# Re-cutting the loads of an in-place channel shuffle: 4, 8, 16, 32 KB in one shared buffer first, 4 KB last

## Chip, cores and metric

One Trainium2 (trn2) chip, one core. The time is the device time of the kernel in microseconds, median over several executions; the times of one kernel mostly differ by some tenths of a per cent, those of the kernel before by up to 1%. The profiler's span, from the first to the last instruction, is about 1.8 us shorter than the timed value of the same execution.

## The reference

The input is 67 MB of float32. Each group of 256 channels is seen as 8 groups of 32 and transposed to 32 times 8. Nothing is computed; every byte is read once and written once.

```python
x = x.reshape(batch, h, w, groups, channels_per_group)   # 16, 64, 64, 8, 32
x = x.transpose(0, 1, 2, 4, 3)
x = x.reshape(batch, h, w, c)
```

## The kernel before

Sizes are rows of 256 floats per partition, so 1 KB each: `16` is 16 KB per partition, 2 MB over 128 partitions. A load fills one of three buffers of 64 KB per partition. DVE (VectorE) copies 8 KB at a time into PSUM, another on-chip memory, in the shuffled order, and ACT (ScalarE) copies it back into the same place. After each 32 KB (or at the end of a smaller load) a store goes out from the same buffer. Loads are issued by SP (SyncE), stores by ACT.

```python
_SIZES = [16, 32] + [64] * 7 + [16]
_BUFS = 3
_STORE = 32
_PIECE = 8
...
    for q in _SIZES:
        buf = pool.tile([P, biggest * c], F32, name="buf")
        nc.sync.dma_start(out=buf[:, : q * c], in_=rows(x_flat, first, q))
        for a in range(0, q, _STORE):
            b = min(a + _STORE, q)
            for k in range(a, b, _PIECE):
                piece = buf[:, k * c : (k + _PIECE) * c]
                bounce = psum.tile([P, _PIECE * c], F32, name="bounce")
                nc.vector.tensor_copy(...)          # shuffle into PSUM
                nc.scalar.copy(out=piece, in_=bounce)
            cols = slice(a * c, b * c)
            nc.scalar.dma_start(
                out=rows(out_flat, first, q)[:, cols], in_=buf[:, cols]
            )
        first += P * q
```

Of the kernel before, what the change touches and what calls it, by code (L numbers as in the profile page):

```python
# [1 line left out]

# [4 lines left out]


F32 = mybir.dt.float32
P = 128  # L10

_SIZES = [16, 32] + [64] * 7 + [16]
_BUFS = 3

_STORE = 32

_PIECE = 8


@with_exitstack  # L20
def kernel(
    ctx: ExitStack,
    tc: tile.TileContext,
    x: bass.AP,
    groups: bass.AP,
    out: bass.AP,
):
    nc = tc.nc
    n, h, w, c = x.shape
    G = int(groups)  # L30
    CPG = c // G
    assert G * CPG == c
    assert sum(_SIZES) * P == n * h * w
    biggest = max(_SIZES)

    x_flat = x.rearrange("b h w c -> (b h w c)")
    out_flat = out.rearrange("b h w c -> (b h w c)")

    pool = ctx.enter_context(tc.tile_pool(name="pool", bufs=_BUFS))
    psum = ctx.enter_context(  # L40
        tc.tile_pool(name="psum", bufs=2, space=bass.MemoryType.PSUM)
    )

    def rows(flat, first, q):

        return flat[first * c : (first + P * q) * c].rearrange("(p f) -> p f", p=P)

    ctx.enter_context(tc.manual_schedule(engines=None))
    first = 0
    for q in _SIZES:  # L50
        buf = pool.tile([P, biggest * c], F32, name="buf")
        nc.sync.dma_start(out=buf[:, : q * c], in_=rows(x_flat, first, q))  # L52
        for a in range(0, q, _STORE):
            b = min(a + _STORE, q)
            for k in range(a, b, _PIECE):
                piece = buf[:, k * c : (k + _PIECE) * c]
                bounce = psum.tile([P, _PIECE * c], F32, name="bounce")
                nc.vector.tensor_copy(  # L58
                    out=bounce.rearrange("p (i j g) -> p i j g", j=CPG, g=G),
                    in_=piece.rearrange("p (i g j) -> p i j g", g=G, j=CPG),  # L60
                )
                nc.scalar.copy(out=piece, in_=bounce)  # L62
            cols = slice(a * c, b * c)
            nc.scalar.dma_start(
                out=rows(out_flat, first, q)[:, cols], in_=buf[:, cols]
            )
        first += P * q


# [1 line left out]
_INS = ['x', 'groups']  # L71
_OUTS = [((16, 64, 64, 256), 'float32')]

_NUMBERS = {'groups': 8}


# [26 lines left out]
```

## Time and profile before

| | before |
|---|---|
| time, median of 3 | 317.65 us (317.52 to 317.97) |
| span of the profiled execution | 317.3 us (that execution was timed at 319.09) |
| DVE / ACT busy | 227.8 / 120.6 us |
| DMA queues, share of 16 engines | 49.6% loads + 49.0% stores |
| bytes moved | 134.24 MB |

### The profile page before, as it was taken

The numbers are of one execution on the slowest core, as the hardware profiler recorded it, in microseconds if no ns is written. First come the engines' busy times: TensorE is split into PE (matmuls) and PEld (weight loads), VectorE is DVE, ScalarE is ACT, GpSimd is POOL, SyncE is SP. The second block draws the span as 40 slices with busy tenths as digits, with TensorE's granted clock in tenths as the row PEclk, the third lists the DMA queues.
The fourth block names the chain that finished last, engine by engine and source line by source line (L and its number), as shares of the span: only waits on it lengthen the run. The fifth ranks groups of instructions, "written<-read, shape, count | busy, mean of one in ns | idle before, by whom it ended". The sixth has DMA issues, their size and how long they took to land.

```text
span 317.3 us, 235 instructions
## 1 busy us (share of the span) xinstructions
DVE 227.8 (72%) x64; ACT 120.6 (38%) x65; POOL 0.2 (0%) x4
## 2 busy tenths in 40 slices
DVE  0979039993999999915999069990799807999600
ACT  0444205552444455421544215442245502455500
POOL 0000000000000000000000000000000000000000
DMA  8998999999999999999999999999999999999995
GB/s 318 413 492 361 456 397 413 446 401 463 401 500 413 401 442 417 508 397 409 430 483 417 397 443 409 475 392 442 439 479 397 425 438 413 446 430 434 438 417 231
DMA packets 3890, 134.24 MB, mean 423 GB/s; under 512 B 432, under 2 KB 432, under 8 KB 432
## 3 DMA queue, kind: packets, MB, share of 16 engines
q1 hardware_dynamic: 1440, 67.11, 49.6%
q10 hardware_dynamic: 2448, 67.11, 49.0%
q14 instruction: 2, 0.02, 0.0%
HBM read 67.11 MB, written 67.11 MB: 423 GB/s over the span
## 4 chain that ended last, share of the span: by engine, by line
DMA 56%; DVE 22%; another core or an unknown queue 12%; ACT 2%; DVEq 1%; issue 1%; SPq 0%
DMA buf<-in_x_dram 34%; DMA out_dram<-buf 22%; DVE bounce L58 22%; ACT buf L62 2%; DVEq L98 1%; SPq L52 0%; DVEq L58 0%
## 5 line engine op out<-in xcount | busy, mean ns | idle before, releaser
L58 DVE COPY bounce<-buf 128x2048 f32<-128x2048 f32 x64 | 227.8, 3637 | 71.2 <-DMA buf<-in_x_dram 71.2
L62 ACT COPY buf<-bounce 128x2048 f32<-128x2048 f32 x64 | 119.4, 1865 | 171.8 <-DVE bounce L58 171.8
L62 ACT ACT_TABLE_LOAD x1 | 1.3, 1283 | 8.4 <-DMA buf<-in_x_dram 8.4
L84 POOL MEMSET const-uint8-127<- 128x1 uint8 x1 | 0.1, 102 | 0.0
L84 POOL MEMSET const-bfloat16-1.0<- 128x1 bf16 x1 | 0.1, 101 | 0.0
L84 POOL MEMSET const-float32-0.0<- 128x1 f32 x1 | 0.1, 98 | 0.2 <-issue 0.2
L84 POOL MEMSET const-float32-1.0<- 128x1 f32 x1 | 0.1, 98 | 0.0
## 6 DMA issues: line engine op xcount, KB each, us to landing
out_dram<-buf ACTq DMA_DIRECT2D x15, 4096.0 KB, 40.4
buf<-in_x_dram SPq DMA_DIRECT2D x2, 2048.0 KB, 13.1
buf<-in_x_dram SPq DMA_DIRECT2D x1, 4096.0 KB, 16.9
out_dram<-buf ACTq DMA_DIRECT2D x2, 2048.0 KB, 21.5
buf<-in_x_dram SPq DMA_DIRECT2D x7, 33.4
```

The source lines that it names most:

```text
L58: nc.vector.tensor_copy(out=bounce.rearrange("p (i j g) -> p i j g", j=CPG, g=G), in_=piece.rearrange("p (i g j) -> p i j g", g=G, j=CPG),)
L62: nc.scalar.copy(out=piece, in_=bounce)
L84: nc = _bacc.Bacc("TRN2", target_bir_lowering=False, num_devices=1)
L98: with _tile.TileContext(nc) as tc:
```

## The change

The intent: begin computing sooner (a 4 KB load lands sooner than one of 16 KB), spend no buffer of its own on each small load, and end with a small piece, so that little is left to compute and store after the last load.

```diff
-_SIZES = [16, 32] + [64] * 7 + [16]
+_SLOTS = [[4, 8, 16, 32]] + [[64]] * 7 + [[4]]
...
-    for q in _SIZES:
+    for parts in _SLOTS:
         buf = pool.tile([P, biggest * c], F32, name="buf")
-        nc.sync.dma_start(out=buf[:, : q * c], in_=rows(x_flat, first, q))
...
+        at = 0
+        pieces = []
+        for q in parts:
+            pieces.append((q, first, at))
+            nc.sync.dma_start(
+                out=buf[:, at * c : (at + q) * c], in_=rows(x_flat, first, q)
+            )
+            first += P * q
+            at += q
+        for q, start, at in pieces:
+            for a in range(0, q, _STORE):
+                b = min(a + _STORE, q)
+                for k in range(a, b, _PIECE):
+                    m = min(_PIECE, b - k)
...                     # the same two copies, of m rows
```

Loads go from 10 to 12 and stores from 17 to 19. The fourth buffer use must now wait for all four stores of the first buffer.

More of the change, by code (lines that the diff above doesn't have):

```diff
@@ L32 @@
     assert G * CPG == c
-    assert sum(_SIZES) * P == n * h * w
-    biggest = max(_SIZES)
+    assert sum(map(sum, _SLOTS)) * P == n * h * w
+    biggest = max(map(sum, _SLOTS))
     x_flat = x.rearrange("b h w c -> (b h w c)")
@@ L49 @@
     first = 0
-    for q in _SIZES:
+    for parts in _SLOTS:
         buf = pool.tile([P, biggest * c], F32, name="buf")
-        nc.sync.dma_start(out=buf[:, : q * c], in_=rows(x_flat, first, q))
-        for a in range(0, q, _STORE):
-            b = min(a + _STORE, q)
-            for k in range(a, b, _PIECE):
-                piece = buf[:, k * c : (k + _PIECE) * c]
-                bounce = psum.tile([P, _PIECE * c], F32, name="bounce")
-                nc.vector.tensor_copy(
-                    out=bounce.rearrange("p (i j g) -> p i j g", j=CPG, g=G),
-                    in_=piece.rearrange("p (i g j) -> p i j g", g=G, j=CPG),
-                )
-                nc.scalar.copy(out=piece, in_=bounce)
-            cols = slice(a * c, b * c)
-            nc.scalar.dma_start(
-                out=rows(out_flat, first, q)[:, cols], in_=buf[:, cols]
-            )
-        first += P * q
+        at = 0
[12 more added lines that the diff above has]
+                    m = min(_PIECE, b - k)
+                    piece = buf[:, (at + k) * c : (at + k + m) * c]
+                    bounce = psum.tile([P, _PIECE * c], F32, name="bounce")
+                    bounce = bounce[:, : m * c]
+                    nc.vector.tensor_copy(
+                        out=bounce.rearrange("p (i j g) -> p i j g", j=CPG, g=G),
+                        in_=piece.rearrange("p (i g j) -> p i j g", g=G, j=CPG),
+                    )
+                    nc.scalar.copy(out=piece, in_=bounce)
+                nc.scalar.dma_start(
+                    out=rows(out_flat, start, q)[:, a * c : b * c],
+                    in_=buf[:, (at + a) * c : (at + b) * c],
+                )
 _INS = ['x', 'groups']
```

## The prediction

> **What bounds the kernel now.** I read the page's share of each engine first, then its strip of 40 slices with the DMA queues, then the chain that ended last, then the waits of the queue that issues loads, and last the busy share of the DMA engines in short windows at both ends.
>
> The page, busy shares, strip and queues:
>
> ```profile
> span 317.3 us, 235 instructions
> DVE 227.8 (72%) x64; ACT 120.6 (38%) x65; POOL 0.2 (0%) x4
> ...
> DMA  8998999999999999999999999999999999999995
> ...
> DMA packets 3890, 134.24 MB, mean 423 GB/s; under 512 B 432, under 2 KB 432, under 8 KB 432
> ...
> q1 hardware_dynamic: 1440, 67.11, 49.6%
> q10 hardware_dynamic: 2448, 67.11, 49.0%
> ```
>
> No compute engine is the bound: DVE is idle for 28% of the span. The DMA strip is full from the first slice to the last but one. The two queues' packets (q1 the loads, q10 the stores) take 49.6 + 49.0 = 98.6% of 16 engines' time, 312.9 us of 317.3. What is not filled is 317.3 - 312.9 = 4.4 us. While busy the engines move 134.24 MB / 312.9 us = 429 GB/s. The kernel has to read 67.11 MB and write 67.11 MB whatever the order, so this number is what the change must be held against.
>
> The chain that ended last names other things too: waits for DVE appear in it with 22%. Its first lines, columns start in us, length in us, what:
>
> ```profile
> 0.73 7.63 DMA buf<-in_x_dram
> 8.36 0.02 issue
> 8.38 7.16 DVE bounce L58 x2
> ...
> 17.46 27.51 DMA out_dram<-buf
> 44.97 0.02 issue
> 44.99 0.03 SPq L52
> ```
>
> This is latency of one small item, and not work that the chip lacked. The 2 MB store issued at 17.46 took 27.51 us to land because it shared the engines with loads already queued. Only then did its buffer come free for the fourth load. The waits of the load queue say the same, 263.3 us in seven waits for stores to land:
>
> ```profile
> SPq L52 <- DMA out_dram<-buf: 263.3, 7, 45.5
> ```
>
> A wait of a queue is a cost only if the DMA engines run dry during it. So the ends decide. Windows, with columns start:end and length, busy DVE, ACT, POOL, clock, DMA share, GB/s:
>
> ```profile
> 0.00:2.00 2.00, 0.00 (x0) 0.00 (x0) 0.20 (x4) 1.00 0.61 115
> 2.00:3.00 1.00, 0.00 (x0) 0.00 (x0) 0.00 (x0) 1.00 0.35 82
> ...
> 4.00:5.00 1.00, 0.00 (x0) 0.00 (x0) 0.00 (x0) 1.00 1.11 475
> ...
> 300.00:305.00 5.00, 0.00 (x0) 0.88 (x1) 0.00 (x0) 1.00 1.05 452
> 305.00:307.00 2.00, 0.00 (x0) 0.00 (x0) 0.00 (x0) 1.00 0.95 410
> ...
> 312.00:313.00 1.00, 0.00 (x0) 0.00 (x0) 0.00 (x0) 1.00 1.03 442
> 313.00:314.00 1.00, 0.00 (x0) 0.00 (x0) 0.00 (x0) 1.00 0.50 213
> 314.00:315.00 1.00, 0.00 (x0) 0.00 (x0) 0.00 (x0) 1.00 0.15 66
> ```
>
> A packet is booked whole where it begins, which is why a share can pass 1.00; I read neighbours together. Compute ends at 300.9 us, when the last 2 MB store is issued. Yet the DMA stays full to 313, twelve microseconds more: about 12.1 x 0.429 = 5.2 MB were still to be moved, of which only 2.1 MB belong to that last store. The tail is a backlog of stores, not an exposed last computation. After 313 only stragglers of the 16 engines remain: the last store's sixteen completions in the trace are spread from 313.8 to 316.4, median 314.1. At the head the first packet starts at 1.72 us.
>
> **What the Trainium skill says.** "DMA: Bandwidth & Descriptors", section "Where 436 GB/s comes from", gives 435.2 GB/s as the ceiling of the 16 ports. The 429 GB/s above is 98.5% of it. "HBM Reference", section "Specifications (TRN2)", says that a core streaming alone measures about 425 GB/s, bounded by its 16 DMA engines; the trace's 423 over the span agrees. "DMA: Bandwidth & Descriptors", section "Queues, rings and completion order", says that each engine takes the queues that have work in turn, one packet at a time. The trace agrees: a packet here is one partition's row, with 8 rows per engine and transfer. The packet records show 0.611 us for 16 KB, 1.213 for 32 KB and 2.418 for 64 KB. Eight 16 KB store packets taken in turn with 64 KB load packets need 8 x (0.611 + 2.418) = 24.2 us, and the store above took 27.51. So in this kernel loads get two thirds of the engines when both queues are full (64 KB against 32 KB), and stores lag.
>
> **The change, part by part.**
>
> *Bytes.* Unchanged: 67.11 MB each way.
>
> *Packets.* Sixteen KB more cost 1.213 - 0.611 = 0.602 us, so 0.611 - 0.602 = 0.009 us of a packet lies beside its bytes. Loads go from 10 to 12 transfers and stores from 17 to 19. That is 4 more transfers of 128 rows and 16 completions each: 512 data packets and 64 completions (recorded at 0.009 us each). On 16 engines: 576 x 0.009 / 16 = 0.32 us more.
>
> *Compute.* DVE now has 63 copies of 128x2048 and two of 128x1024, the same elements and one instruction more. DVE stays near 228 us and ACT near 121, both far below 313. One instruction's fixed cost is hidden.
>
> *Head.* Six loads are issued in a row at some 0.33 us each, 188 KB per partition, 24.6 MB, which is 57 us of DMA work. The first load of 0.5 MB lands near 3.5 us instead of 8.36 (estimate: 1.72 + about 1.2 to 1.8), so compute begins 5 us sooner and the first store goes out near 7 us instead of 17.46. The DMA was full in that stretch anyway, so nothing is gained from it: the same engines now carry stores earlier and the loads later.
>
> *First buffer.* This is the part that could do harm. The fourth buffer's load waited for the 16 KB store, which landed at 44.97. Now it waits until all four stores of the first buffer have landed. The 32 KB load lands near 23 us (7.9 MB plus about 1.2 MB of stores, 9.1 / 0.429 = 21 us, after 1.7). Its four DVE pieces (4 x 3.56) and the last ACT copy (1.86) give a store issued near 39. The stores before it: the 8 KB one, issued near 11, done near 31 (eight packets of 0.3 us in turn with load packets of 1.2 and then 2.4), the 16 KB one 24 us later, 55. From there the 32 KB store takes turns with 64 KB loads, 3.63 us per pair. The loads of the two following buffers run out at about (24.6 + 6.4) / 0.429 + 1.7 = 74 us; by then five of the eight pairs are gone, and three packets of 1.2 us are left: the buffer is free near 77 us, against 45. Would the engines run dry in between? The second buffer's load lands near 46, so its two 32 KB stores are issued near 46 + 14.2 + 1.9 = 62 and 76.5. They wait in the queue behind the 32 KB store. So at 74 to 77 there are stores to move, and then loads come again. Cost: 0.
>
> *Middle.* A buffer of 64 KB moves 16.78 MB, 39.1 us of DMA, against 8 x 3.56 = 28.5 us of DVE. DVE has over 10 us to spare per buffer, as the pauses of 10 to 12 us before each buffer in the trace show. Cost: 0.
>
> *Tail.* Before, DVE begins the last 64 KB load at 263.4 and about 50.7 us x 0.429 = 21.7 MB are moved after that. Of these 8.4 MB are its own stores and 4.2 MB the 16 KB part both ways, so 9.1 MB were backlog of earlier stores. After, the same backlog plus 8.4 plus 1.05 MB is 18.5 MB, 43 us of DMA. The last store is issued 28.5 + 1.8 + 1.0 + about 0.5 = 32 us after that landing, so some 11 us of backlog lie before it. The shorter last piece is hidden: gain 0. The stragglers (2.3 us from the median engine to the last) stay of the same kind, but their size is chance to me: between 1 and 3.5 us.
>
> Sum: 317.65 + 0.32 + 0 + 0 + 0 = 318.0 us.
>
> **Rivals.** First, that the ends count as the chain suggests. The last piece falls by 12 KB per partition, 1.5 DVE pieces (5.3 us) and 1.57 MB of store (3.7 us), 9 us in all, which would give 309. Against it stands the full DMA from 4 to 313, and the floor: first packet 1.72, busy 312.9 + 0.3, and about 1.3 us from the last data packet (316.05 in the trace) to the end make 316.2 even with perfectly even engines. Even if every slowed packet were gone, 3458 packets at their usual durations sum to about 310.5 us per engine, so a floor of 313.5. Faster by over 2% (under 311.3) is closed off.
>
> Second, that the buffer wait takes the place of the head's gain: if the queues run dry for the 3 us from 74 to 77, or the second buffer's stores come 5 us late, the time is 321 to 323. For it speaks a first release 32 us later; against it the backlog worked out above, which has 14 us to spare (store issued near 62, needed near 77).
>
> Third, that small packets cost more than their 0.009 us. The first packets in the trace took up to 1.89 us instead of 0.611. If the start cost is per packet, smaller first loads pay it on less data; I put it at up to 0.7 us more, 318.7.
>
> Fourth, that the lag of the slowest engine changes. Removing it wholly gives 316.2; doubling it gives 320.
>
> **Range and chances.** The centre is 318.0 less a little for a shorter last store, which leaves less to spread: I say 317.9. The fourth rival sets the width, so 316.4 to 319.5. Within 2% means 311.3 to 324.0. Chances: faster 0.01, within 2% 0.96, slower 0.03, nearly all of it from the second rival.
>
> **What would show it.** Right: the DMA strip full from the second to the last but one slice, queue shares summing to 98 to 99% with about 4466 packets, the first DVE copy near 3.5 us, the fourth buffer's load issued near 77 us, and DMA still near 430 GB/s for about 10 us after the last store's issue. Wrong: a slice of the strip at 7 or lower between 60 and 90 us (second rival), DMA idle while DVE works on the last buffer (first rival), or a queue share that rises by over 1% with the same bytes (third).

## The result

The changed kernel takes 317.33 us (median of 4, 317.07 to 317.66) against 317.58 for the kernel before (median of 4, 317.34 to 317.97). The ratio is 0.9991, with a 95% interval of 0.9974 to 1.0009. A ratio here is the mean time of one kernel's runs over that of the other's of the same rounds, so it is not quite the ratio of the medians. Executions over 1.5% slower than the fastest of the same kernel are left out of the means. The page of the changed kernel, the lines that answer to those of before:

```profile
span 315.4 us, 247 instructions
DVE 227.9 (72%) x65; ACT 120.8 (38%) x66; POOL 0.2 (0%) x4
...
DMA  8999999899998999999999999999899998999996
...
DMA packets 4466, 134.24 MB, mean 426 GB/s; under 512 B 496, under 2 KB 496, under 8 KB 1008
...
q1 hardware_dynamic: 1728, 67.11, 49.7%
q10 hardware_dynamic: 2736, 67.11, 49.4%
```

The bytes are the same, the strip is full again, and the queues add to 99.1%, 312.5 us of 315.4. The span is 1.9 us shorter, but most of that is no gain of the change: the profiled execution of before was itself 1.4 us slower than its kernel's median. Of the last store's sixteen completions, those of before are spread over 2.6 us (313.8 to 316.4), those of the changed kernel over 1.0 (313.5 to 314.5); the two medians, 314.1 and 313.9, differ by 0.2. Per engine, on average, packets fill 312.9 us of the span of before and leave 4.4 empty; in the changed kernel they fill 312.5 and leave 2.8.

What moved is visible in the timeline. Columns: start us, length us, engine, line, operation, count, and in brackets the idle time before it:

```profile
4.09 1.88 DVE L69 COPY bounce<-buf 128x1024 f32<-128x1024 f32 x1 [4.09 <-DMA buf<-in_x_dram]
...
7.04 0.37 ACTq L74 DMA_DIRECT2D out_dram<-buf  x1
...
39.70 0.34 ACTq L74 DMA_DIRECT2D out_dram<-buf  x1
46.42 56.86 DVE L69 COPY bounce<-buf 128x2048 f32<-128x2048 f32 x16 [8.65 <-DMA buf<-in_x_dram]
...
62.60 0.34 ACTq L74 DMA_DIRECT2D out_dram<-buf  x1
...
76.79 0.34 ACTq L74 DMA_DIRECT2D out_dram<-buf  x1
```

The first copy begins 4.3 us sooner, the first store 10.4 us sooner, as intended. The load queue alone, asked for 60 to 110 us, shows the price, the fourth buffer's load:

```profile
79.62 0.33 SPq L56 DMA_DIRECT2D buf<-in_x_dram  x1
```

It goes out at 79.62, where before the fourth buffer's load went out at 45. Neither counts, because the engines were moving bytes throughout. Windows, with columns start:end and length, busy DVE, ACT, POOL, clock, DMA share, GB/s:

```profile
60.00:65.00 5.00, 5.00 (x3) 2.62 (x2) 0.00 (x0) 1.00 1.21 524
65.00:70.00 5.00, 5.00 (x2) 2.98 (x2) 0.00 (x0) 1.00 0.73 315
70.00:75.00 5.00, 5.00 (x3) 1.97 (x2) 0.00 (x0) 1.00 1.09 472
75.00:80.00 5.00, 5.00 (x2) 3.31 (x2) 0.00 (x0) 1.00 1.05 452
...
300.00:305.00 5.00, 0.00 (x0) 0.00 (x0) 0.00 (x0) 1.00 1.00 433
...
309.00:310.00 1.00, 0.00 (x0) 0.00 (x0) 0.00 (x0) 1.00 0.99 426
310.00:311.00 1.00, 0.00 (x0) 0.00 (x0) 0.00 (x0) 1.00 0.99 426
311.00:312.00 1.00, 0.00 (x0) 0.00 (x0) 0.00 (x0) 1.00 0.65 279
```

A packet is booked where it begins, so the 0.73 of 65 to 70 belongs with the 1.21 of the five microseconds before it. The packet records, sampled every 0.05 us from 60 to 90, show never fewer than sixteen packets under way. At the tail the last store, of 0.5 MB, is issued at 299.87. In the windows the DMA share stays near 1 for 11 us more; in the records sixteen packets are under way until 313, 13 us after that issue.

### The profile page after: what moved, and what is told of

Read it like the earlier page. It is cut to its first block, busy times and chain, and to the rows that moved or that the text cites. A ratio compares the mean times of both kernels' runs of the same rounds, so it can differ in the third digit from the quotient of the medians.

```text
span 315.4 us, 247 instructions
## 1 busy us (share of the span) xinstructions
DVE 227.9 (72%) x65; ACT 120.8 (38%) x66; POOL 0.2 (0%) x4
## 2 busy tenths in 40 slices
DMA packets 4466, 134.24 MB, mean 426 GB/s; under 512 B 496, under 2 KB 496, under 8 KB 1008
## 4 chain that ended last, share of the span: by engine, by line
DMA 50%; DVE 23%; another core or an unknown queue 18%; ACT 2%; issue 1%; SPq 1%; ACTq 0%; DVEq 0%
DMA buf<-in_x_dram 35%; DVE bounce L69 23%; DMA out_dram<-buf 16%; ACT buf L73 2%; SPq L56 1%; ACTq L74 0%; DVEq L69 0%; ACTq L73 0%
## 5 line engine op out<-in xcount | busy, mean ns | idle before, releaser
L69 DVE COPY bounce<-buf 128x2048 f32<-128x2048 f32 (+1 forms) x65 | 227.9, 3586 | 70.3 <-DMA buf<-in_x_dram 68.3
L73 ACT COPY buf<-bounce 128x2048 f32<-128x2048 f32 (+1 forms) x65 | 119.5, 1839 | 174.9 <-DVE bounce L69 174.4
## 6 DMA issues: line engine op xcount, KB each, us to landing
buf<-in_x_dram SPq DMA_DIRECT2D x1, 2048.0 KB, 10.5
```

The lines of the kernel that those rows point to most:

```text
L69: nc.vector.tensor_copy(out=bounce.rearrange("p (i j g) -> p i j g", j=CPG, g=G), in_=piece.rearrange("p (i g j) -> p i j g", g=G, j=CPG),)
```

## The experiments

Theory A says that the transfers of the 16 DMA engines are the only path, full from first packet to last, so that neither end nor any wait counts while they are full. Theory B says that the small pieces did gain at the ends and that the later release of the first buffer, or the like, took it back. Each ratio compares a run with runs of the kernel before on its chip; differences in us sometimes set runs of two chips side by side. Whether the engines themselves or something behind them limits what they move was not tested; the argument doesn't need it.

**Without computing.** Both copies are taken out, so the output is wrong. The transfers stay.

```diff
-                for k in range(a, b, _PIECE):
-                    ...   # both copies
```

> The changed kernel without its DVE and ACT copies (a wrong result on purpose): the same loads, stores, sizes and buffers. Theory A (16 DMA engines are full from the first packet to the last, nothing else is on the path): the same 317.3 us within 1.5 us, DMA queue shares summing to 98 to 99%. Theory B (the shorter first and last pieces did gain some 9 us at the ends, and the later release of the first buffer gave it back as a wait): with no compute there is nothing to wait for between load and store, so the time falls by 5 us or more, to 312 or below.

Measured: 316.91 us, ratio to before 0.9962 (0.9921 to 1.0002).

```profile
span 314.6 us, 91 instructions
...
DMA  8999989999997999999999999999799999999997
...
q1 hardware_dynamic: 1728, 67.11, 49.8%
q10 hardware_dynamic: 2736, 67.11, 49.5%
```

With 228 us of DVE and 121 of ACT gone, the span shrinks by 0.8 us and the shares still add to 99.3%. No order of these pieces could have gained more by hiding computation better. This speaks plainly for A.

**No small pieces at all.** Eight loads of 64 KB, run twice.

```diff
-_SLOTS = [[4, 8, 16, 32]] + [[64]] * 7 + [[4]]
+_SLOTS = [[64]] * 8
```

> No small pieces at all: eight loads of 64 KB per partition in three buffers, first and last too. First DVE copy near 22 us instead of 4.1, first store near 38 instead of 7.0, last store 4 MB instead of 0.5 MB. Theory A: the three loads keep the engines full until about 60 us, and after the last landing some 9 MB of older stores plus 8.4 MB of its own are left, 41 us, against 40.2 us for computing and storing it: just enough. Time 316.5 to 318.5 us, ratio to before 0.995 to 1.003. Theory B: 18 us later at the head and about 9 at the tail, so 325 to 345 us.

> Eight loads of 64 KB once more, on the same chip as the run above, because its first median (319.11 us) lay 0.6 above the expected range while its ratio lay inside. Theory A: 0 to 2 us above the changed kernel. If it is 3 us or more above, the missing small pieces do cost something.

Measured: 319.11 us, ratio 1.0024 (0.9978 to 1.007), then 318.55 us, ratio 0.9992 (0.9957 to 1.0028). The first median lies 0.6 us above the stated range, the ratio inside it. On the second chip it is 1.05 us above the changed kernel (317.50 there), inside the 0 to 2 that A allowed. The first DVE copy starts very late and it does not matter:

```profile
22.68 39.10 DVE L69 COPY bounce<-buf 128x2048 f32<-128x2048 f32 x11 [22.68 <-DMA buf<-in_x_dram]
```

Computing begins 18.6 us later than in the changed kernel and costs about 1 us. In the packet records that microsecond is slower packets: in the second run 3.3 us per engine beyond the usual duration (the median) of each packet size, against 1.7 in the changed kernel on that chip. Having 1008 packets fewer gives 0.5 of it back.

**Two buffers instead of three**, for both kernels.

```diff
-_BUFS = 3
+_BUFS = 2
```

> The changed kernel with two buffers of 64 KB. Theory A says that only empty DMA queues cost time; with two buffers the engines should run dry while one buffer is computed on and the other waits for its stores. Estimate 325 to 345 us, DMA queue shares 90 to 96% of the longer span, with slices at 7 or lower in the strip. If the time stays at 317, two buffers suffice and the idle time needs another explanation.

> The kernel before with two buffers of 64 KB, for the pair with the run above. Theory A: also 325 to 345 us. Theory B (the shared first buffer costs a wait that its early start pays back): with two buffers the shared first buffer's late release can no longer be hidden, so the changed kernel should be slower than this one by 5 us or more; theory A expects the two within 4 us of each other, since a first buffer released late was also filled with more.

Measured: 347.72 us for the changed kernel (ratio 1.0933), 349.21 for the one before (1.0992). The strip and the shares of the changed kernel with two buffers:

```profile
DMA  8999988989998989979998989979999989994957
...
q1 hardware_dynamic: 1728, 67.11, 48.0%
q10 hardware_dynamic: 2736, 67.11, 45.2%
```

Here the engines do run dry: 93.2% of 344.8 us leaves 23.4 us empty, against 2.8 with three buffers. The other 8.7 us of the loss are slower packets. This is what a real buffer wait looks like. I had set the range too low by 3 to 4 us, because I counted only the empty time. The shared first buffer is not worse than the old cut even here, which is against B.

**Every DVE copy done twice**, for both kernels, with a right result. Now DVE is the bound (458 us busy), and the ends must count.

```diff
                     nc.vector.tensor_copy(... same copy ...)
+                    nc.vector.tensor_copy(... same copy ...)
```

> The changed kernel with every DVE copy done twice (right result): 456 us of DVE work, more than the 313 of DMA, so DVE becomes the bound. The ends must then count: first copy starts near 4.1, last small copy and ACT copy and 0.5 MB store after DVE's end: 4.1 + 456 + 1 + 1.2 + about 3 = 465 to 468 us, plus 2 that timing adds. If DVE pauses for loads early on, up to 475.

> The kernel before with every DVE copy done twice: 8.4 + 456 + 1.9 + 5 for the 2 MB store + about 2.5 = 474 to 477 us, plus 2. Theory A: slower than the changed kernel with double copies by 6 to 11 us, the gain that the small pieces were made for, which shows only where the DMA engines are not full. If the two are equal, the small pieces do not shorten the ends even then.

Measured: 477.43 us for the changed kernel, 479.30 for the one before. The gain is there, but 1.9 us and not 6 to 11. That was a miss (and the two times lie 2.4 and 0.3 us above the most that was expected, 475 and 479). The timelines say where the rest of the gain is. The changed kernel with double copies:

```profile
462.16 1.88 DVE L73 COPY bounce<-buf 128x1024 f32<-128x1024 f32 x1
462.23 0.34 ACTq L78 DMA_DIRECT2D out_dram<-buf  x1
464.07 1.01 ACT L77 COPY buf<-bounce 128x1024 f32<-128x1024 f32 x1 [1.87 <-DVE bounce L73]
465.12 0.34 ACTq L78 DMA_DIRECT2D out_dram<-buf  x1
```

The kernel before with double copies:

```profile
455.69 0.34 ACTq L68 DMA_DIRECT2D out_dram<-buf  x1
...
464.53 3.60 DVE L62 COPY bounce<-buf 128x2048 f32<-128x2048 f32 x1
468.17 1.86 ACT L66 COPY buf<-bounce 128x2048 f32<-128x2048 f32 x1 [5.32 <-DVE bounce L62]
470.06 0.34 ACTq L68 DMA_DIRECT2D out_dram<-buf  x1
```

DVE ends at 464.04 against 468.13, 4.1 us sooner, which is the gain of the head. From there to the end of the span (475.5 and 477.3) the changed kernel takes 11.4 us and the one before 9.1. The small last store of the changed kernel stands behind a 4 MB store issued 2.9 us earlier; in the kernel before, the last 4 MB store was issued 14.4 us before the last one and is gone. A small last piece after a large one shortens the computing and leaves the large store exposed.

**A graded end**, with double and with single copies, to test that reading.

```diff
-_SLOTS = [[4, 8, 16, 32]] + [[64]] * 7 + [[4]]
+_SLOTS = [[4, 8, 16, 32]] + [[64]] * 6 + [[32, 16, 8, 8], [4]]
```

> The double-copy kernel with the last large load replaced by 32, 16, 8, 8 KB in the last shared buffer, then 4 KB. It asks why the double-copy pair differed by 1.8 us and not by 6 to 11. Theory: the change gained 4.4 us at the head, but at the tail its 0.5 MB store stood behind a 4 MB store issued 2.9 us before it (462.23 and 465.12), so 11.4 us passed between the last copy's start and the end against 9.1 in the kernel before. With graded stores the last 0.5 MB store finds the engines nearly free: DVE and ACT end near 465.2, the store takes 3 to 3.5, so a span of 468 to 470 and a time of 470 to 472 us, 6 us below the double-copy version of the change. If the time stays at 477, the tail is not what took the gain.

> The same graded end with single copies, the kernel as the user would run it. Theory A: the DMA engines are full to the end whatever the last store's size; three loads and two stores more are 5 x 144 packets, 0.4 us: 317 to 318.5 us, ratio to before 0.997 to 1.004. If a graded tail were worth here what the double-copy runs say, 6 us, it would be 311.

Measured with double copies: 470.62 us, 6.8 below the change and 8.7 below the kernel before, both with double copies. These are times of two chips; the plain kernel before took 318.58 us on this one and 317.68 on the other, so the chip doesn't explain the gain. The stores at the end are now small:

```profile
455.01 0.34 ACTq L78 DMA_DIRECT2D out_dram<-buf  x1
...
462.19 0.34 ACTq L78 DMA_DIRECT2D out_dram<-buf  x1
...
464.04 1.01 ACT L77 COPY buf<-bounce 128x1024 f32<-128x1024 f32 x1 [1.88 <-DVE bounce L73]
465.08 0.34 ACTq L78 DMA_DIRECT2D out_dram<-buf  x1
```

DVE and ACT end at the same time as before the grading, and the span ends at 468.7, 3.6 us after the last store's issue. So the whole 6.8 us came after the last issue, from what stood in front of the last store. With single copies the same cut gives 317.53 us (ratio 0.9963, 0.9933 to 0.9994; the time is inside the range, the ratio 0.0007 below it), where the changed kernel gave 317.33 and 317.50: a gain of 6.8 us where DVE is the bound is none where the DMA engines are.

**Loads of 8 KB packets**, to see the one term of the sum that was not zero.

```diff
-            nc.sync.dma_start(out=buf[:, at * c : (at + q) * c], in_=rows(x_flat, first, q))
+            for r in range(0, q, 8):
+                e = min(r + 8, q)
+                nc.sync.dma_start(out=buf[:, (at + r) * c : (at + e) * c],
+                                  in_=rows(x_flat, first, q)[:, r * c : e * c])
```

> The changed kernel with each load cut into loads of 8 KB per partition (packets of 8 KB instead of up to 64; same buffers, same stores). Transfers on the load queue rise from 12 to 65, so 53 x 128 data packets and 53 x 16 completions more: 7632 x 0.009 / 16 = 4.3 us. Theory A with the packet term: 321 to 322.5 us. If packets cost nothing beside their bytes: 317.3. If stores now win the turns and loads starve, over 325 with gaps in the strip.

Measured: 322.61 us, ratio 1.0153 (1.0119 to 1.0186), 5.3 us above the changed kernel's first median. The page counts 12099 packets, 7633 more (7632 of the loads and one of another queue). In the records the usual 8 KB packet takes 0.309 us and a completion 0.009, which makes 3.7 us more per engine, and another 1.5 us are packets slower than usual. The packet term is real, somewhat under the expected 4.3; the total is 0.1 us above the range.

**One 64 KB store per large load.**

```diff
-_STORE = 32
+_STORE = 64
```

> The changed kernel with one 64 KB store per large load instead of two of 32 KB: 7 x 144 packets fewer, 0.57 us less by the packet term. But the first bytes of a buffer go out 14.2 us later, when all eight pieces are done. Theory A: if the queues stay filled 316.8; if they run dry at the tail, where the last 8.4 MB store needs 19.6 us alone after DVE's end, against 10 us of backlog, up to 10 us more, 325. I expect the latter, with the DMA idle in the tail or before it.

Measured: 334.13 us, ratio 1.0503 (1.047 to 1.0537). The direction was right, the size a miss: up to 325 was expected. The timeline and the windows of the tail:

```profile
280.00 30.27 DVE L69 COPY bounce<-buf 128x2048 f32<-128x2048 f32 x9 [11.32 <-DMA buf<-in_x_dram]
...
310.38 0.34 ACTq L74 DMA_DIRECT2D out_dram<-buf  x1
```

```profile
290.00:295.00 5.00, 5.00 (x3) 2.58 (x2) 0.00 (x0) 1.00 1.03 446
295.00:300.00 5.00, 5.00 (x2) 3.02 (x2) 0.00 (x0) 1.00 0.07 26
300.00:305.00 5.00, 5.00 (x3) 1.93 (x2) 0.00 (x0) 1.00 0.00 0
305.00:310.00 5.00, 5.00 (x2) 3.31 (x2) 0.00 (x0) 1.00 0.00 0
310.00:315.00 5.00, 0.27 (x1) 1.36 (x2) 0.00 (x0) 1.00 0.98 419
```

While DVE works on the last buffer the engines stand still for some 14 us, because nothing may go out before all eight pieces are done. Over the whole span 17.9 us are empty, 15.0 more than in the changed kernel; the remaining 2.8 us of the loss are slower packets, less what the smaller number of packets saves. I had set the gap at 10 us or less: I worked from the changed kernel's tail with its backlog and its earlier half store. The last large load also landed 12 us later (280.0 against 267.9); loads and stores were both 64 KB packets here, so an even share of the turns would explain that, but it was not tested by itself. Of all single-copy runs with three buffers this is the one in which the order counts, and it counts through empty engines.

**The change once more**, in more rounds.

> The changed kernel once more, in five rounds beside the kernel before, since the first comparison left 0.1% open and the runs before scattered from 317.3 to 320.4 us. Theory A: ratio within 0.995 to 1.002, any difference being how far the slowest of the 16 engines lags and not the order of the pieces. If the small pieces gain something real at the ends, the ratio should be below 0.99.

Measured: 317.50 us (317.03 to 317.83), ratio 0.9958 (0.9925 to 0.9991). The interval just excludes 1. What differs is the scatter of the kernel before: over all the rounds 19 of its 40 timed runs are above 318.0 us, up to 320.43 among the fast ones, while no run of the change or of the graded version (16 in all) is above 317.93. In the one profile of before, an execution of 319.09 us, the last completions are spread over 2.6 us; in the change's two profiles over 1.0 and 0.9. So the lag of the slowest engine may be what scatters, and the cut may make it rarer, but one profile does not show that; it stays open. It is 0.4%.

## Why the prediction was right

- The bound. Right: queue shares of 99.1% were predicted as 98 to 99%, the packets as about 4466 and counted 4466. Taking out all computing moved the time by 0.4 us. That a gain of over 2% was closed off holds, but the two floors mixed up span and time: 316.2 and 313.5 are counted from the first instruction, so they are spans, and were set beside times, which are 1.8 us longer. The second floor, 315.3 us as a time, still closes off anything under 311.3. The first is 318.0 as a time, and the medians of both kernels in the first comparison lie below it: it came from the slower execution of before, with 313.2 us of packets where the changed kernel had 312.5. The low end of the range, 316.4, came from that mixed-up floor; that it reached down to the result, 317.33, is partly luck.
- The head. The first load landed at 3.3 to 3.7, as set; the first copy began at 4.09, the first store was issued near 7 as predicted (7.04). The step "nothing is gained from it" holds: the cut with a first copy at 22.68 costs about 1 us.
- The first buffer. Its release was set near 77 us and the load that follows went out at 79.62; the second buffer's stores were set near 62 and 76.5 and were issued at 62.60 and 76.79. The queues did not run dry. The way there was worked out wrongly, though. The 8 KB store landed at 42 us and not near 31, because it first waited for the 4 KB store (landed at 21); the 16 KB store landed at 67 and not at 55; the six loads were through at 70 and not at 74. So the 32 KB store's eight rows went out after the last row of the loads (begun at 67.1) and not in turn with them. The end came out near because the engines were full all the while: by my estimate from the prediction's own rate, six loads and four stores are 32.5 MB, and 32.5 / 0.429 + 1.7 = 77.5 us in whatever order.
- The packets. The term of 0.32 us shows in the packet records (usual durations sum to 310.5 us per engine before and 310.8 after) but not in the totals; enlarged thirteenfold it came out at 3.7 us against 4.3. The third rival's extra start cost did not come: slowed packets of the small first loads (16 and 32 KB before, 4 to 32 KB after) cost 0.88 us per engine before and 0.84 after.
- The tail. "Some 11 us of backlog" before the last store: about 5.9 MB were still to be moved at its issue, 5.4 without its own, which is 12.5 us. The sum of 18.5 MB after the last large load's landing was 19.7 in the records. The shorter last piece was hidden as predicted.
- What it did not see. The page of before came from an execution 1.4 us slower than its median, and the width of the range was taken from its stragglers. The centre, 317.9, is 0.6 us too high; it stands on the median of before, 317.65, plus the packets. The records of the two profiles show 0.7 us per engine less of slowed packets after the change (1.8 against 2.5), for which the sum had no term; with one profile of before, that may be chance.
- The reading of the first rival, 9 us at the ends, was itself too generous. Where DVE is the bound, the change is worth 1.9 us and not 9, since the store in front of the last one was left out of it. This did not touch the prediction.
- Two small slips: the 22% of the chain is DVE's work and not waits for it, and 429 of 435.2 is 98.6%.

## What to carry to other kernels

Add up the DMA queues' shares first: at 98% and more, a new cut of loads and stores had next to nothing to gain, however long the waits in the chain look. It can still lose: by its packets (1.5% with loads of 8 KB), or by letting the engines run dry (5% with 64 KB stores). To settle it in one run, take out the computing and keep the transfers. Where computing is the bound, grade the end step by step: a small last store behind a large one waits for the large one. And keep stores small enough that something goes out while the last buffer is still being computed on.

## What the Trainium skill lacked or had wrong

- "DMA: Bandwidth & Descriptors", section "Queues, rings and completion order", describes packets of some 9 to 17 descriptors. In this case's records a turn is a single row of one partition, up to 64 KB: from 22 to 39 us of the profile of before, some sixteen 64 KB rows of a load and sixteen 16 KB rows of a store begin in every 3.0 us, as many as there are engines. So the turns are that coarse: 0.611 us for 16 KB, 1.213 for 32, 2.418 for 64. That the row size thereby sets the share of each queue follows from the turns; no page says it.
- The same page, section "Rules for kernel authors", asks for at least 1 MiB per DMA for the most bandwidth. Here loads cut to 8 KB per partition (1 MiB each) cost 1.5% with the same buffers and stores; the records show 0.007 to 0.009 us per packet beside its bytes (0.309 us for 8 KB, 0.611 for 16, 1.213 for 32).
- No page mentions that the first packets of a load can take longer. In the changed kernel with two buffers, six loads of 64 KB began on empty engines, and the first sixteen packets of each took 0.58 to 0.77 us longer (median) than the usual 2.418. These make 4.1 of the 10.5 us per engine that all slowed packets added there, against 1.8 in the changed kernel. Empty engines are not the whole reason: in the second run with eight loads of 64 KB, the third and the fourth load began on full engines, and their first sixteen packets took 0.87 and 1.27 us longer. The cause is open.
